# Order hints for a planned kernel: the second tile's tail products behind the first's, a shorter log1p, and a fixed order of the first transfers

## The chip, the core and the metric

The kernel runs on one core of a Trainium2 chip, in one launch. The metric is the device time of that launch in microseconds (us). Five engines work side by side and meet by semaphores: TensorE (PE; its weight loads are shown as PEld), VectorE (DVE), ScalarE (ACT), GpSimd (POOL) and SyncE (SP), whose queue issues every transfer from memory here.

## What is computed

Two transformer blocks run one after the other over a sequence of 256 positions of width 1024, which the kernel holds as two tiles of 128 rows (t = 0 and t = 1). All arithmetic is float32.

```python
def first_block(x, ...):                       # two layers
    for layer in range(2):
        hn = rmsnorm(h, gains[0])
        mix = mixer_ab(hn, ...) if layer == 0 else mixer_c(hn, ...)
        h = h + rmsnorm(mix, gains[1])
        hn = rmsnorm(h, gains[2])
        ff = square(relu(hn @ w_up)) @ w_down
        h = h + rmsnorm(ff, gains[3])
        h = h + sigmoid(h @ w_ple_gate) * (p @ w_ple)

def second_block(x, mem, ...):                 # two layers
    for l in range(2):
        h = rmsnorm(x) @ w_in                  # five kinds of attention
        ... decay = cumsum(log_sigmoid(fox_f + fox_b_f)) ...
        x = x + concat(o_a, o_b, o_c, o_d, o_e) @ w_o
        xn = rmsnorm(x)
        x = x + (silu(causal_dwconv(xn @ w_gate)) * (xn @ w_up)) @ w_down
```

In `mixer_ab` the gates need softplus and log-sigmoid, both through log(1 + e^-|y|).

## The kernel before, in words

Each weight matrix is read in blocks of up to 1 MB into one of two `raw` buffers. `block` splits a block into a rounded part `hi` and a rest `lo` (ACT or DVE copies `hi`, DVE subtracts to get `lo`, in four parts each), which live in four buffers of each kind. A float32 product is then three PE products: `tmm` multiplies a 128-column slice of the block with the transposed activations `aTh`, `aTl` of both tiles at once (256 columns), `nmm` multiplies one tile's activations with 512 columns of the block, for one or two PSUM banks (two banks are the two halves of a 1024-wide result).

Nothing runs in the order in which the code is written. `Recorder.note` collects every instruction with the instructions it depends on; `Recorder.order` ranks them and `arrange` places them on the engines by an estimated cost of each and by waits between engines (`LAG`); `issue` writes each engine's instructions out in that order. On the chip each engine goes through its list in order and waits where an operand isn't there. So a dependency that is added in the recorder adds no wait on the chip: it changes the order alone.

The stages, with the names that matter below:

- Start: `h[0]`, `h[1]` (the two tiles of x), a gain row `g0`, the constants `cf` (its first 128 columns are the identity, with which PE transposes), the columns `cols`, the masks `cb`, `rows` and `pos` are loaded. `normed_T` scales the tiles (DVE, ACT, POOL) and transposes them into `aTh`/`aTl`. The first products are those of the blocks `w0g` (the gates) and `w0t` (ten blocks).
- `mixer_ab`: `gates` makes decay factors from the w0g product on DVE and ACT; `delta` solves triangular systems by a long chain of small products; `w0n` and at last the output matrix `w0o` follow.
- `stream` runs a list `seq` of (block, tile) steps. For an output matrix the list is `tail_lagged(n, tail)`: both tiles for the first n - tail blocks, then the last `tail` blocks for tile 0, then the same blocks for tile 1. `done` is called when a tile's last product is recorded, and spawns what follows it. The gate matrices `wg` use `lagged(4, 2)`, where tile 1 runs two blocks behind tile 0.
- `pre_ff1` (after w0o and w1o): mean square of the tile's result, residual, scaling, four transposes of each half into `aT`. `ff1`: the blocks `wu` and `wd` by turns; when a tile's `wd` sums are complete, `post` does mean square, root, residual and the transposes of `h`; then come the products of `wg`.
- `mixer_c` with `w1n`, `w1o`; `ff1` again; `mixers2` (five attentions, blocks `wi`, `wm`, memory products `wk`, output `wo`) and `ff2` (`fg`, `fu`, `fd`), twice.

In names of the trace and of the orders a number is the tile buffer's; almost every instruction is recorded by one line (L613).

Of the kernel before, what the change touches and what calls it, by code (L numbers as in the profile page):

```python
# [15 lines left out]
OP = mybir.AluOpType  # L16
AX = mybir.AxisListType.X

P = 128
# [53 lines left out]
CF = {}  # L73
# [184 lines left out]
class Recorder:  # L258
# [7 lines left out]
           "act": {"pe": 271, "act": 160, "dve": 142, "pool": 155, "sp": 1220},  # L266
           "dve": {"pe": 270, "act": 128, "dve": 127, "pool": 155, "sp": 1220},
           "pool": {"pe": 200, "act": 90, "dve": 69, "pool": 97, "sp": 1220},
           "sp": dict.fromkeys(("pe", "act", "dve", "pool", "sp"), 2050)}

    def __init__(self, nc):
        self.engines = {"pe": nc.tensor, "act": nc.scalar, "dve": nc.vector, "pool": nc.gpsimd, "sp": nc.sync}
        self.ops, self.pools, self.tile_pool, self.seen = [], {}, {}, {}
        self.run = None


    @contextmanager
    def together(self, share=1):

        self.run = []  # L280
        yield
        op = self.ops[self.run[0]]
        op.cost = op.cost / share + 200 * (share > 1)
        self.run = None

    def engine(self, name):
        rec = self
# [53 lines left out]
    def note(self, eng, call, args, kwargs):  # L341
        op = Op()
        op.eng, op.call, op.args, op.kwargs = eng, call, args, kwargs
        op.preds, op.succs, op.tiles, op.alt, op.more = {}, [], [], None, []
        op.table = self.TABLES.get(args[2], 0) if call == "activation" and args[2] != AF.Copy else None
        isap = lambda x: hasattr(x, "tensor") or hasattr(x, "tag_meta")
        outs = [kwargs[k] for k in ("out", "accum_out") if k in kwargs and isap(kwargs[k])]
        ins = [v for k, v in kwargs.items() if k not in ("out", "accum_out") and isap(v)]
        rest = [a for a in args if isap(a)]
        if "out" not in kwargs:  # L350
            outs.append(rest.pop(0))
        op.cost, op.lag = self.price(op, outs[-1], rest + ins), self.LAG[eng]
        if self.run:
            i = self.run[0]
            first = self.ops[i]
            first.more.append((call, args, kwargs))
            first.cost += op.cost
            op = first
        else:
            i = len(self.ops)  # L360
            self.ops.append(op)
            if self.run is not None:
# [298 lines left out]
def program(ctx, tc, A, out, dbg=None):  # L661
# [157 lines left out]
    def stream(name, items, acts, kpb, halves_, n, seq, done, before=None):  # L819


        first, last = {}, {}
        for t in range(2):
            for i, tt in seq:
                if tt == t:
                    first.setdefault((items[i][0], t), i)
                    last[items[i][0], t] = i
        banks, live = {}, {}
        w = halves_ * n
        for i, t in seq:  # L830
            c, b, k0 = items[i]
            if i not in live:
                live[i] = block(name, b, kpb, w)
            if before is not None:
                before(items[i], t)
            if (c, t) not in banks:
                banks[c, t] = [acc() for _ in range(halves_)]
            hi, lo = live[i]
            for j in range(kpb):
                nmm(banks[c, t], acts(t, k0 + j), hi[:, j, :], lo[:, j, :],  # L840
                    first[c, t] == i and j == 0, last[c, t] == i and j == kpb - 1, n)
                if (j + 1) * 3 * halves_ % 6 == 0:
                    loom.step()
            if last[c, t] == i:
                done(c, t, banks.pop((c, t)))

    def a_T(t, k):
# [248 lines left out]
        put(values_T(pTs, v, ns, heads))  # L1096


    def mixer_ab(end):
        nab = gain(14)  # L1100
        done = {}
        st = {}

        def gates(bank):
# [6 lines left out]
            act.activation(e, e, AF.Exp)  # L1111
            dve.tensor_scalar(u, e, 1.0, None, op0=OP.add)
            act.activation(ln, u, AF.Ln)
            dve.tensor_scalar(u, u, -1.0, None, op0=OP.add)
            dve.scalar_tensor_tensor(z, u, 0.0, e, op0=OP.is_equal, op1=OP.mult)
            dve.tensor_scalar(u, u, 1e-30, None, op0=OP.max)
            dve.reciprocal(u, u)
            dve.tensor_tensor(ln, ln, e, op=OP.mult)
            dve.tensor_tensor(ln, ln, u, op=OP.mult)
            dve.tensor_tensor(ln, ln, z, op=OP.add)  # L1120
            dve.scalar_tensor_tensor(ln, y, 0.0, ln, op0=OP.max, op1=OP.add)
            ca = small(1)
            act.activation(ca, col("alog"), AF.Exp)
# [256 lines left out]
                done[2 + hp, t] = pair_T(flat(m))  # L1380


        hi, lo = block("w0g", 0, 8, P)
        gbank = wk(2)
        tmm(gbank, hi, lo, 1)
        loom.spawn(gates(gbank), "gates")
# [4 lines left out]

        st["nrm"] = wk()
        for bi in W0T:
            hi, lo = block("w0t", bi, 8, 256)
            ps = wk(2)
            tmm(ps, hi, lo)
            if bi >= 6:
# [3 lines left out]
            if bi == 3:  # L1401
                loom.join(*[("conv", i) for i in range(4)], "gates")
                for hp in range(2):
                    g2 = small(4)
                    dve.tensor_copy(g2[:, 0:2], st["eg", 1][:, 2 * hp : 2 * hp + 2])
                    dve.tensor_copy(g2[:, 2:4], st["eg", 1][:, 2 * hp : 2 * hp + 2])
                    st["eg2", hp] = g2
                loom.spawn(norms(), "norms")

        def nat_done(c, t, banks):  # L1410
            b = banks[0]
# [26 lines left out]
            loom.join(*([("B", j - 2)] if j >= 2 else [("A", j, t)]))  # L1438

        items = [(0, j, 2 * j) for j in (2, 3, 0, 1)]  # L1440
        stream("w0o", items, lambda t, k: done[k // 2, t](k % 2), 2, 2, 512, tail_lagged(4, 2), end, before)


    def mixer_c(r, end):
# [32 lines left out]
        def nat_done(c, t, banks):  # L1477
# [5 lines left out]
        stream("w1o", items, lambda t, k: done[k // 2, t](k % 2), 2, 2, 512, tail_lagged(4, 2), end,  # L1483
               lambda it, t: loom.join(("C", it[1], t)))


# [209 lines left out]
    def mixers2(l, r, e, mem, tab, lam, end):  # L1696
# [70 lines left out]
        def forget():  # L1767
# [8 lines left out]
            dve.tensor_scalar(u, u, -1.0, None, op0=OP.add)  # L1776
            dve.scalar_tensor_tensor(z, u, 0.0, e, op0=OP.is_equal, op1=OP.mult)
            dve.tensor_scalar(u, u, 1e-30, None, op0=OP.max)
            dve.reciprocal(u, u)
            dve.tensor_tensor(ln, ln, e, op=OP.mult)  # L1780
            dve.tensor_tensor(ln, ln, u, op=OP.mult)
            dve.tensor_tensor(ln, ln, z, op=OP.add)
            dve.scalar_tensor_tensor(lg, y, 0.0, ln, op0=OP.min, op1=OP.subtract)
            yield
            yield
# [246 lines left out]
        return tabC, tabS, cos_, sin_  # L2032


    sp.dma_start(out=h[0], in_=A["x"][0])
    g0 = gain(0)
    sp.dma_start(out=cf, in_=A["cf"])
    sp.dma_start(out=h[1], in_=A["x"][1])
    loom.spawn(normed_T(0, g0))
    loom.spawn(normed_T(1, g0))  # L2040
    sp.dma_start(out=cols, in_=A["cols"])
    sp.dma_start(out=cb, in_=A["cb"])
    sp.dma_start(out=rows, in_=A["rows"])
    sp.dma_start(out=pos, in_=A["pos"])
    loom.drain()
    tabC, tabS, cos_, sin_ = tables()


    e = [None, None]
# [5 lines left out]
            g2.append(gain(2))  # L2055
        loom.spawn(pre_ff1(0, t, banks, g1[0], g2[0], e), ("pre", 0, t))

    mixer_ab(out0)
    loom.drain()
    dumph("m0")  # L2060

# [99 lines left out]
```

## Time and profile before

| | |
|---|---|
| time, median of 3 runs | 1399.25 us (1395.28 to 1400.75) |
| the profiled execution's own time | 1395.2 us |
| its span, first to last instruction | 1393.4 us |
| mean granted TensorE clock | 0.996 of 2.4 GHz |
| PE busy | 1359.3 us, 98% of the span |
| DVE, ACT, POOL busy | 998.3, 786.4, 56.4 us |

The profile is of one execution. The time of an execution is 1.8 us more than its span, which covers only the program's instructions. PE's busy time is a union of modelled intervals; products overlap in the engine, so the time that a product costs is read from one start to the next.

### The profile page before, as it was taken

The numbers are of one execution on the slowest core, as the hardware profiler recorded it, in microseconds if no ns is written. First come the engines' busy times: TensorE is split into PE (matmuls) and PEld (weight loads), VectorE is DVE, ScalarE is ACT, GpSimd is POOL, SyncE is SP. The second block draws the span as 40 slices with busy tenths as digits, with TensorE's granted clock in tenths as the row PEclk, the third lists the DMA queues.
The fourth block names the chain that finished last, engine by engine and source line by source line (L and its number), as shares of the span: only waits on it lengthen the run. The fifth ranks groups of instructions, "written<-read, shape, count | busy, mean of one in ns | idle before, by whom it ended". The sixth has DMA issues, their size and how long they took to land.

```text
span 1393.4 us, 23108 instructions
## 1 busy us (share of the span) xinstructions
PE 1359.3 (98%) x8768; PEld 1199.4 (86%) x8774; DVE 998.3 (72%) x2417; ACT 786.4 (56%) x1800; POOL 56.4 (4%) x93
## 2 busy tenths in 40 slices
PE   6999999999999999999999999999999999999998
PEld 6899889999787799998787877999998877899997
DVE  6994876666677876566789798575767999576664
ACT  6665554444554854445576596454546679364443
POOL 0000210000010010000020000000001000000000
PEclk9999999999999999999999999999999999999999
DMA  8332354445543364445555243454545523345553
GB/s 329 134 126 99 114 212 182 182 184 194 212 147 141 139 224 179 185 182 194 207 193 206 91 142 132 152 211 153 212 155 205 187 90 99 144 153 210 182 189 114
DMA packets 36400, 236.36 MB, mean 170 GB/s; under 512 B 4160, under 2 KB 4416, under 8 KB 10176
## 3 DMA queue, kind: packets, MB, share of 16 engines
q1 hardware_dynamic: 36288, 234.88, 46.4%
q8 instruction: 69, 1.13, 0.3%
q14 instruction: 43, 0.35, 0.1%
HBM read 233.82 MB, written 1.05 MB: 169 GB/s over the span
## 4 chain that ended last, share of the span: by engine, by line
PE 88%; DVE 6%; ACT 4%; issue 1%; DMA 1%; SPq 0%; POOLq 0%; POOL 0%; ACTq 0%; DVEq 0%
PE ps L613 88%; ACT w L613 3%; DVE w L613 3%; DVE s L613 2%; DMA cf<-in_cf 1%; DVE lo L613 1%; ACT hi L613 1%; DVE h L613 0%; ACT L613 0%; SPq L613 0%; POOLq L2157 0%; DVE hi L613 0%; ACT aTh L613 0%; POOL s L613 0%; ACTq L613 0%
## 5 line engine op out<-in xcount | busy, mean ns | idle before, releaser
L613 ACT ACTIVATE hi<-raw 128x512 fp32r<-128x512 f32 (+1 forms) x793 | 437.6, 620 | 297.7 <-PE ps L613 244.9
L613 DVE TENSOR_TENSOR lo<-raw,hi 128x512 fp32r<-128x512 f32 (+1 forms) x844 | 526.0, 678 | 51.4 <-ACT hi L613 48.1
L613 PE MATMUL ps<-hi,w 128*128 128x512 f32 (+1 forms) x1272 | 379.1, 395 | 0.5 <-ACT w L613 0.5
L613 PE MATMUL ps<-aTl,hi 128*128 128x256 f32 x1256 | 316.7, 280 | 0.0
L613 PE MATMUL ps<-aTh,hi 128*128 128x256 f32 x1256 | 316.3, 281 | 0.0
L613 PE MATMUL ps<-aTh,lo 128*128 128x256 f32 x1256 | 312.5, 280 | 0.0
L613 PEld LDWEIGHTS ps<-hi,w 128*128 128x128 f32 x1272 | 225.2, 188 | 36.1 <-issue 1.9
L613 PEld LDWEIGHTS ps<-aTh,hi 128*128 128x128 f32 x1256 | 224.8, 188 | 9.4 <-ACT hi L613 0.4
L613 PEld LDWEIGHTS ps<-aTl,hi 128*128 128x128 f32 x1256 | 225.1, 188 | 8.3 <-issue 0.4
L613 PEld LDWEIGHTS ps<-aTh,lo 128*128 128x128 f32 x1256 | 223.6, 189 | 9.9 <-DVE lo L613 1.0
L613 PE MATMUL ps<-lo,w 128*128 128x512 f32 (+1 forms) x636 | 205.9, 393 | 0.0
L613 ACT ACTIVATE w<-ps 128x512 f32<-128x512 f32 (+3 forms) x261 | 128.3, 535 | 130.4 <-PE ps L613 119.9
L613 PE MATMUL ps<-hi,aTh 128*128 128x512 f32 (+2 forms) x480 | 148.4, 366 | 3.7 <-ACT w L613 2.5
L613 DVE CAST hi<-raw 128x512 fp32r<-128x512 f32 x51 | 21.8, 427 | 177.8 <-PE ps L613 177.8
L613 PE MATMUL ps<-lo,aTh 128*128 128x512 f32 (+2 forms) x480 | 147.2, 365 | 0.0
L613 PE MATMUL ps<-hi,aTl 128*128 128x512 f32 (+2 forms) x480 | 147.2, 365 | 0.0
L613 ACT ACTIVATE w<-w 128x512 fp32r<-128x512 f32 (+5 forms) x143 | 74.9, 535 | 95.3 <-DVE w L613 93.0
L613 PEld LDWEIGHTS ps<-lo,w 128*128 128x128 f32 x636 | 112.6, 188 | 17.0 <-issue 0.8
L613 PE MATMUL ps<-cf,w 128*128 128x128 f32 (+1 forms) x572 | 94.7, 279 | 17.4 <-DMA cf<-in_cf 10.6
L613 PE MATMUL ps<-w,w 128*64 128x128 f32 (+10 forms) x912 | 109.5, 299 | 0.6 <-ACT w L613 0.5
L613 PEld LDWEIGHTS ps<-w,w 128*128 128x128 f32 (+4 forms) x912 | 88.7, 171 | 20.0 <-ACT w L613 7.4
L613 PEld LDWEIGHTS ps<-hi,aTh 128*128 128x128 f32 x480 | 86.8, 190 | 16.2 <-ACT w L613 2.8
(105 smaller groups left out, 1143.8 us busy)
## 6 DMA issues: line engine op xcount, KB each, us to landing
raw<-in_wu SPq DMA_DIRECT2D x32, 1024.0 KB, 4.8
raw<-in_wd SPq DMA_DIRECT2D x32, 1024.0 KB, 5.0
raw<-in_fg SPq DMA_DIRECT2D x22, 1024.0 KB, 4.8
raw<-in_fu SPq DMA_DIRECT2D x22, 1024.0 KB, 4.8
raw<-in_fd SPq DMA_DIRECT2D x22, 1024.0 KB, 4.8
raw<-in_wi SPq DMA_DIRECT2D x20, 1024.0 KB, 4.8
raw<-in_w0t SPq DMA_DIRECT2D x10, 1024.0 KB, 5.5
raw<-in_wo SPq DMA_DIRECT2D x10, 1024.0 KB, 4.8
```

The source lines that it names most:

```text
L613: getattr(self.engines[op.eng], call)(*args, **kwargs)
```

## The change

Four things are edited. (1) The recorder gets `behind(*ops)`: whatever is recorded inside depends, for the order, on the named instructions. In `stream` with a single group of columns, PE products of tile 1 recorded after tile 0's last step stand behind the instruction recorded last at that point. The tails of w0o and w1o are 3 blocks long, not 2. (2) log1p by another formula: with u = 1 + e, log(u) + (u - 1 - e)(e/2 - 1), without a reciprocal. (3) The first transfers stand in a fixed order: the identity's columns of `cf` by themselves, x, the gain, w0g, the first w0t, `cols`, the rest of `cf`; `cb` after the second w0t, `rows`, `pos` and the gain of mixer_ab after the w0t blocks. (4) The rotary tables are recorded after mixer_ab.

```diff
-           "sp": dict.fromkeys(("pe", "act", "dve", "pool", "sp"), 2050)}
+           "sp": {"pe": 2050, "act": 2050, "dve": 2050, "pool": 2050, "sp": 0}}
...
+    @contextmanager
+    def behind(self, *ops, only=None):
+
+        self.hold, self.only = ops, only
+        yield
+        self.hold = ()
+
+    def last(self):
+        return len(self.ops) - 1
...
+            if self.hold and self.only in (None, eng):
+                op.preds.update(dict.fromkeys(self.hold, True))
...
             for j in range(kpb):
-                nmm(banks[c, t], acts(t, k0 + j), hi[:, j, :], lo[:, j, :],
-                    first[c, t] == i and j == 0, last[c, t] == i and j == kpb - 1, n)
+                with rec.behind(*(ended if t else ()), only="pe"):
+                    nmm(banks[c, t], acts(t, k0 + j), hi[:, j, :], lo[:, j, :],
+                        first[c, t] == i and j == 0, last[c, t] == i and j == kpb - 1, n)
                 if (j + 1) * 3 * halves_ % 6 == 0:
                     loom.step()
             if last[c, t] == i:
+                if t == 0 and len(last) == 2:
+                    ended.append(rec.last())
                 done(c, t, banks.pop((c, t)))
...
-            dve.tensor_scalar(u, u, -1.0, None, op0=OP.add)
-            dve.scalar_tensor_tensor(z, u, 0.0, e, op0=OP.is_equal, op1=OP.mult)
-            dve.tensor_scalar(u, u, 1e-30, None, op0=OP.max)
-            dve.reciprocal(u, u)
-            dve.tensor_tensor(ln, ln, e, op=OP.mult)
-            dve.tensor_tensor(ln, ln, u, op=OP.mult)
-            dve.tensor_tensor(ln, ln, z, op=OP.add)
+
+            dve.scalar_tensor_tensor(u, u, -1.0, e, op0=OP.add, op1=OP.subtract)
+            dve.tensor_scalar(z, e, 0.5, -1.0, op0=OP.mult, op1=OP.add)
+            dve.tensor_tensor(u, u, z, op=OP.mult)
+            dve.tensor_tensor(ln, ln, u, op=OP.add)
...
-        stream("w0o", items, lambda t, k: done[k // 2, t](k % 2), 2, 2, 512, tail_lagged(4, 2), end, before)
+        stream("w0o", items, lambda t, k: done[k // 2, t](k % 2), 2, 2, 512, tail_lagged(4, 3), end, before)
...
-    sp.dma_start(out=h[0], in_=A["x"][0])
-    g0 = gain(0)
-    sp.dma_start(out=cf, in_=A["cf"])
-    sp.dma_start(out=h[1], in_=A["x"][1])
+
+    at = CF["ident"][0]
+    sp.dma_start(out=cf[:, at : at + P], in_=A["cf"][:, at : at + P])
+    with rec.behind(rec.last()):
+        sp.dma_start(out=h[0], in_=A["x"][0])
+    with rec.behind(rec.last()):
+        sp.dma_start(out=h[1], in_=A["x"][1])
+    with rec.behind(rec.last()):
+        g0 = gain(0)
...
+    for name, w in (("w0g", P), ("w0t", 256)):
+        with rec.behind(load[-1], only="sp"):
+            first.append(block(name, 0, 8, w))
```

The same four lines replace the seven in `gates` (256 columns) and in `forget` (8 columns, once in each layer of the second block).

The order of the transfers on SP at the start, before. `raw` is a weight block; with two `raw` buffers the third `raw` row waits until a buffer is read out.

```order
L613 DMA h_81<-in_x 128x1024
L613 DMA h_82<-in_x 128x1024
L613 DMA gb_88<-in_gb 128x1024
L613 DMA raw_142<-in_w0t 128x2048
L613 DMA cf<-in_cf 128x449
L613 DMA raw_117<-in_w0g 128x1024
L613 DMA cols<-in_cols 128x263
L613 DMA cb<-in_cb 128x3456
L613 DMA gb_116<-in_gb 128x1024
L613 DMA gb_489<-in_gb 128x1024
L613 DMA raw_148<-in_w0t 128x2048
```

And of the change:

```order
L627 DMA cf<-in_cf 128x128
L627 DMA h_81<-in_x 128x1024
L627 DMA h_82<-in_x 128x1024
L627 DMA gb_88<-in_gb 128x1024
L627 DMA raw_107<-in_w0g 128x1024
L627 DMA raw_110<-in_w0t 128x2048
L627 DMA cols<-in_cols 128x263
L627 DMA cf<-in_cf 128x321
L627 DMA gb_480<-in_gb 128x1024
L627 DMA gb_481<-in_gb 128x1024
L627 DMA raw_138<-in_w0t 128x2048
```

The identity went from fifth place to first, the w0g block from sixth to fifth, ahead of the first w0t block, and the masks `cb` left the stretch.

PE's order at the end of the first `ff1`, before: ps_537 and ps_538 are tile 0's sums of the down products, ps_539 and ps_540 tile 1's; a row `ps<-cf,h_82 x4` is four transposes of tile 1's h, `h_81` of tile 0's; ps_757 is the first bank of the gate products that follow.

```order
L613 MATMUL ps_539<-hi_725,w_720 128x512
L613 MATMUL ps_537<-hi_725,w_719 128x512
L613 MATMUL ps_538<-hi_725,w_719 128x512
L613 MATMUL ps_537<-lo_726,w_719 128x512
L613 MATMUL ps_537<-hi_725,w_720 128x512
L613 MATMUL ps_538<-lo_726,w_719 128x512
L613 MATMUL ps_538<-hi_725,w_720 128x512
L613 MATMUL ps_744<-cf,h_82 128x128 x4
L613 MATMUL ps_745<-cf,h_82 128x128 x4
L613 MATMUL ps_735<-cf,h_81 128x128 x4
L613 MATMUL ps_757<-hi_747,aTh 128x512
```

And of the change; the line of dots stands for 28 further products of ps_539 and ps_540, and no other row.

```order
L627 MATMUL ps_538<-hi_725,w_720 128x512
L627 MATMUL ps_537<-hi_725,w_720 128x512
L627 MATMUL ps_539<-hi_711,w_697 128x512
L627 MATMUL ps_540<-hi_711,w_697 128x512
...
L627 MATMUL ps_539<-hi_725,w_719 128x512
L627 MATMUL ps_540<-hi_725,w_719 128x512
L627 MATMUL ps_735<-cf,h_81 128x128 x4
L627 MATMUL ps_539<-lo_726,w_719 128x512
L627 MATMUL ps_540<-lo_726,w_719 128x512
L627 MATMUL ps_539<-hi_725,w_720 128x512
L627 MATMUL ps_540<-hi_725,w_720 128x512
L627 MATMUL ps_736<-cf,h_81 128x128 x4
```

Before, both tiles' sums end within nine products and the transposes stand right behind; in the change 32 products of tile 1 stand between tile 0's last product and its transposes. At the end of the second `ff1` it is the same with other numbers.

PE's order at the end of w0o, before: ps_476 and ps_477 are the halves of tile 0's result, ps_478 and ps_479 of tile 1's; ps_529 to ps_534 are products of `wp`, the block that comes next; the transposes of w_498 need tile 0's residual and scaling.

```order
L613 MATMUL ps_477<-hi_487,w_367 128x512
L613 MATMUL ps_478<-lo_488,w_386 128x512
L613 MATMUL ps_478<-hi_487,w_386 128x512
L613 MATMUL ps_479<-hi_487,w_386 128x512 x2
L613 MATMUL ps_479<-lo_488,w_386 128x512
L613 MATMUL ps_479<-hi_487,w_386 128x512
L613 MATMUL ps_533<-hi_527,w_524 128x512
...
L613 MATMUL ps_530<-hi_527,w_525 128x512
L613 MATMUL ps_500<-cf,w_498 128x128 x4
```

And of the change: ps_467 and ps_468 are tile 0's halves (the last product of ps_468 stands 80 products and four transposes further up), ps_469 and ps_470 are tile 1's.

```order
L627 MATMUL ps_467<-hi_478,w_358 128x512
L627 MATMUL ps_470<-hi_478,w_377 128x512
L627 MATMUL ps_469<-lo_479,w_377 128x512
L627 MATMUL ps_469<-hi_478,w_377 128x512
L627 MATMUL ps_470<-lo_479,w_377 128x512
L627 MATMUL ps_470<-hi_478,w_377 128x512
L627 MATMUL ps_529<-hi_527,w_524 128x512
...
L627 MATMUL ps_534<-hi_527,w_525 128x512
L627 MATMUL ps_491<-cf,w_489 128x128 x4
```

Tile 0's last product is followed by 24 products before the transposes in the one, by 29 in the other. The instruction recorded last, which the held products stand behind, is a product of one half (ps_468); the other half (ps_467) still lies among tile 1's products.

## Rows read from the trace of the kernel before

**Rows 1.** The page: its head, and part 1 (busy time, share, instructions).

```profile
span 1393.4 us, 23108 instructions
PE 1359.3 (98%) x8768; PEld 1199.4 (86%) x8774; DVE 998.3 (72%) x2417; ACT 786.4 (56%) x1800; POOL 56.4 (4%) x93
```

**Rows 2.** Sum of three windows of the attention stages: 440:480, 780:860, 1120:1180; busy us.

```profile
sum 180.00, PE 176.18 PEld 135.65 DVE 162.24 ACT 148.35 POOL 1.83; mean PE 58.73 PEld 45.22 DVE 54.08 ACT 49.45 POOL 0.61
```

**Rows 3.** Timeline of SP at the start: start, duration, what is issued.

```profile
0.72 0.86 SPq L613 DMA_DIRECT2D h<-in_x  x2
...
13.13 0.33 SPq L613 DMA_DIRECT2D raw<-in_w0t  x1
```

**Rows 4.** DMA issues of 0 to 14 us: KB each, us from issue to landing.

```profile
cf<-in_cf SPq DMA_DIRECT2D x1, 224.5 KB, 7.9
```

**Rows 5.** DMA issues of 12 to 14 us.

```profile
raw<-in_w0t SPq DMA_DIRECT2D x1, 1024.0 KB, 6.6
```

**Rows 6.** The page, part 6: weight blocks in the middle of the program.

```profile
raw<-in_wu SPq DMA_DIRECT2D x32, 1024.0 KB, 4.8
```

**Rows 7.** Timeline of PE, 0 to 14.5 us; in brackets idle before and releaser.

```profile
10.64 3.65 PE L613 MATMUL ps<-cf,w 128*128 128x128 f32 x16 [10.64 <-DMA cf<-in_cf]
13.94 0.68 PE L613 MATMUL ps<-aTh,hi 128*128 128x256 f32 x2
```

**Rows 8.** Timeline of PE, 57 to 61.6 us, where the gates' chain begins.

```profile
56.83 0.28 PE L613 MATMUL ps<-aTh,hi 128*128 128x256 f32 x1
...
57.06 0.28 PE L613 MATMUL ps<-aTh,lo 128*128 128x256 f32 x1
...
59.93 1.13 PE L613 MATMUL ps<-w,cf 128*128 128x256 f32 x4 [0.87 <-ACT w L613]
```

**Rows 9.** Timeline of DVE at the start and in the gates.

```profile
7.57 2.74 DVE L613 SCALAR_TENSOR_TENSOR w<-h,s,gb 128x512 f32<-128x512 f32 x4 [1.94 <-DMA gb<-in_gb]
...
51.79 1.73 DVE L613 RECIPROCAL w<-w 128x256 f32<-128x256 f32 x1
```

**Rows 10.** Timeline of ACT at the second w0t block and in the gates.

```profile
19.74 2.20 ACT L613 ACTIVATE hi<-raw 128x512 fp32r<-128x512 f32 x4 [4.35 <-DMA raw<-in_w0t]
...
47.55 1.28 ACT L613 ACT_TABLE_LOAD   x1
48.84 0.42 ACT L613 ACTIVATE w<-w 128x256 f32<-128x256 f32 x1
```

**Rows 11.** Timeline of PE at the end of w0o.

```profile
191.37 1.07 PE L613 MATMUL ps<-hi,w 128*128 128x512 f32 x4
192.28 0.61 PE L613 MATMUL ps<-lo,w 128*128 128x512 f32 x2
192.73 0.61 PE L613 MATMUL ps<-hi,w 128*128 128x512 f32 x2
195.14 0.63 PE L613 MATMUL ps<-cf,w 128*128 128x128 f32 x4 [1.79 <-DVE w L613]
```

**Rows 12.** Timeline of PE at the ends of both ff1.

```profile
377.12 0.39 PE L613 MATMUL ps<-hi,w 128*128 128x512 f32 x1
380.86 1.51 PE L613 MATMUL ps<-cf,h 128*128 128x128 f32 x6 [3.35 <-issue]
...
680.09 0.39 PE L613 MATMUL ps<-hi,w 128*128 128x512 f32 x1
683.89 2.37 PE L613 MATMUL ps<-cf,h 128*128 128x128 f32 x10 [3.41 <-DVE h L613]
```

**Rows 13.** Windows of PE behind three waits: us, PE busy, granted clock, DMA share, GB/s.

```profile
380.86:388.00 7.14, 7.14 (x28) 0.61 0.23 73
683.89:688.00 4.11, 4.11 (x21) 0.64 0.55 191
...
759.56:764.00 4.44, 4.44 (x19) 1.00 1.00 387
```

**Rows 14.** Timeline of PE in the first attention layer.

```profile
759.56 0.50 PE L613 MATMUL ps<-hi,aTh 128*128 128x512 f32 x1 [2.52 <-ACT w L613]
```

More of the change, by code (lines that the diff above doesn't have):

```diff
@@ L273, in __init__ @@
         self.ops, self.pools, self.tile_pool, self.seen = [], {}, {}, {}
-        self.run = None
+        self.run, self.hold, self.loads = None, (), []
     @contextmanager
@@ L361, in note @@
             self.ops.append(op)
+            if self.hold and self.only in (None, eng):
+                op.preds.update(dict.fromkeys(self.hold, True))
+            if eng == "sp":
+                self.loads.append(i)
             if self.run is not None:
@@ L827, in stream @@
                     last[items[i][0], t] = i
[L828 removed]
+        banks, live, ended = {}, {}, []
         w = halves_ * n
@@ L1096, in attention, with mixer_ab @@
         put(values_T(pTs, v, ns, heads))
-    def mixer_ab(end):
-        nab = gain(14)
+    def mixer_ab(first, end):
         done = {}
@@ L1380, in mlstm @@
                 done[2 + hp, t] = pair_T(flat(m))
-        hi, lo = block("w0g", 0, 8, P)
+        hi, lo = first[0]
         gbank = wk(2)
@@ L1393, in mixer_ab @@
         for bi in W0T:
-            hi, lo = block("w0t", bi, 8, 256)
+            hi, lo = first[1] if bi == 0 else block("w0t", bi, 8, 256)
+            if bi == 1:
+                with rec.behind(rec.loads[-1]):
+                    sp.dma_start(out=cb, in_=A["cb"])
             ps = wk(2)
@@ L1408, in mixer_ab @@
                 loom.spawn(norms(), "norms")
+        with rec.behind(rec.loads[-1]):
+            sp.dma_start(out=rows, in_=A["rows"])
+            sp.dma_start(out=pos, in_=A["pos"])
+            nab = gain(14)
         def nat_done(c, t, banks):
@@ L1482, in mixer_c @@
         items = [(0, j, 2 * j) for j in range(4)]
-        stream("w1o", items, lambda t, k: done[k // 2, t](k % 2), 2, 2, 512, tail_lagged(4, 2), end,
+        stream("w1o", items, lambda t, k: done[k // 2, t](k % 2), 2, 2, 512, tail_lagged(4, 3), end,
                lambda it, t: loom.join(("C", it[1], t)))
@@ L1775, in forget @@
             act.activation(ln, u, AF.Ln)
[L1776 to L1782, printed above, removed]
+            dve.scalar_tensor_tensor(u, u, -1.0, e, op0=OP.add, op1=OP.subtract)
+            dve.tensor_scalar(z, e, 0.5, -1.0, op0=OP.mult, op1=OP.add)
+            dve.tensor_tensor(u, u, z, op=OP.mult)
+            dve.tensor_tensor(ln, ln, u, op=OP.add)
             dve.scalar_tensor_tensor(lg, y, 0.0, ln, op0=OP.min, op1=OP.subtract)
@@ L2032, in tables @@
         return tabC, tabS, cos_, sin_
-    sp.dma_start(out=h[0], in_=A["x"][0])
-    g0 = gain(0)
-    sp.dma_start(out=cf, in_=A["cf"])
-    sp.dma_start(out=h[1], in_=A["x"][1])
+    at = CF["ident"][0]
[6 more added lines that the diff above has]
+        g0 = gain(0)
+    load = [rec.last()]
     loom.spawn(normed_T(0, g0))
     loom.spawn(normed_T(1, g0))
[L2041 to L2044, printed above, removed]
+    first = []
+    for name, w in (("w0g", P), ("w0t", 256)):
+        with rec.behind(load[-1], only="sp"):
+            first.append(block(name, 0, 8, w))
+        load.append(rec.loads[-1])
+    with rec.behind(load[-1]):
+        sp.dma_start(out=cols, in_=A["cols"])
+    with rec.behind(rec.last()):
+        sp.dma_start(out=cf[:, at + P :], in_=A["cf"][:, at + P :])
     loom.drain()
-    tabC, tabS, cos_, sin_ = tables()
     e = [None, None]
@@ L2056, in out0 @@
         loom.spawn(pre_ff1(0, t, banks, g1[0], g2[0], e), ("pre", 0, t))
-    mixer_ab(out0)
+    mixer_ab(first, out0)
+    tabC, tabS, cos_, sin_ = tables()
     loom.drain()
```

## The prediction

> **What bounds the kernel now.** The head of the page comes first: PE is busy for 1359.3 of 1393.4 us, no other engine for more than 998.3 [rows 1]. The reader is to see that only about 34 us of the span are PE waits, so a change of order can win no more than these waits, and what they do to the clock; the products themselves are the same in both programs. The next view is therefore PE's timeline, read for the bracketed waits. The larger ones stand in five kinds of place.
>
> - The start: transposes wait until 10.64 for `cf`, the first product begins at 13.94 [rows 7].
> - The gates' chain after 57 us: 0.87 and some smaller ones [rows 8].
> - The end of w0o: the last products start at 192.73, the transposes at 195.14 [rows 11]. A product of 512 columns takes (192.28 − 191.37)/4 = 0.2275, so the two end at 193.19 and PE waits 1.95.
> - The ends of the two `ff1`: the last product, issued at 377.12, ends at 377.35, the transposes start at 380.86, a wait of 3.51; the same at 680.09 and 683.89, a wait of 3.57 [rows 12]. Behind them PE has work at once but not the clock: the granted mean is 0.61 over 7.14 us and 0.64 over 4.11 [rows 13], the lower level of 1.2 GHz for most of it. At 0.61, 7.14 us do the work of 4.36, so 2.78 are lost; at 0.64, 1.48. Behind the wait of 2.52 at 759.56 [rows 14] the clock stayed at 1.00 [rows 13], so a shorter wait there lost only itself.
> - The attention stages: in 180 us PE is busy for 176.18 [rows 2], 3.8 idle in many small pieces, with DVE at 90%.
>
> **The change part by part.** The sum is made against the profiled execution's own 1395.2 us.
>
> *Second tile behind the first.* At the first `ff1`, tile 0's last product and its transposes stood six products apart; they now have 32 between them, 32 × 0.2275 = 7.28 us. The chain (square, root, residual) needed 6 × 0.2275 + 3.51 = 4.87 from tile 0's last product. So tile 0's wait goes, and with it the reason for the half clock. What is late next is tile 1: its last product is followed by four of tile 0's transposes (about 0.1 each at the full clock, half of the 3.30/16 at the start [rows 7]) and 16 products of `wg` (3.64), some 4.04 us in all. With 4.87 needed 0.9 remains. Term: −3.5 − 2.8 + 0.9 = −5.4. Bounds: −6.3 if one tile's chain alone is shorter than two that share DVE and ACT, −2 if tile 1's wait is longer and the clock goes down again. At the second `ff1` eight products of cover become 28 (6.37 us), need 8 × 0.2275 + 3.57 = 5.39; tile 1 then has 21 products and four transposes, 5.18, so 0.2 remains: −3.6 − 1.5 + 0.2 = −4.9 (−5 to −2).
>
> At the end of w0o the edit does less than it says: only one half of tile 0's result is finished early. The other half ends 29 products before the transposes instead of 24: 6.60 us of cover against a need of 24 × 0.2275 + 1.95 = 7.41, so at most 0.8 of the 1.95 remains, and less if the early half's share of the chain is done by then. I take −1.5 (−1.95 to 0). At w1o no wait of this kind stood before, at the ends of `wo` I see the same number of products or a few less behind the chain; 0 (0 to +0.3).
>
> In the attention stages, the products still left on PE when the last attention operation comes fall from 48 to 34 (w1o) and from 36 to 27 (each wo): more of them are spread among the attention's operations, which fills some of the 3.8 idle. I take −1.5 (−3.8 to 0). The wait of 2.52 at 759.56 is for a copy that ACT has queued behind other work; nothing in the edits is aimed at it, but the order around it shifts: 0 (−2.5 to +3).
>
> *log1p.* DVE loses the reciprocal, 1.73 [rows 9], and two operations of three in balance, about 2.4 us once, and far less where eight columns are wide. The chain of the gates gets shorter by as much. It is hidden: DVE works on it while PE runs w0t's products until 57.17. In the new order it stands some 10 us earlier and the small products of `delta` follow with fewer large ones between them, so waits like the 0.87 [rows 8] can become less or more. 0 (−1.6, all waits of this place gone, to +2.5, as many again and half). The trace has two table loads fewer to come (1.28 each), on ACT, which PE rarely waits for.
>
> *Transfers.* Before, `cf` landed 7.9 us after its issue [rows 4], ready 10.5, and the transposes began at 10.64. DVE had begun scaling at 7.57, when the gain landed, and its four scalings last 2.74, to 10.31 [rows 9]. With the identity ahead, everything behind it is issued one slot later, 0.43 (half of the 0.86 for the two h) [rows 3]: the gain lands at about 7.9 to 8.0, scaling starts then, the first transposes can start a scaling later, at about 8.7, but the last scaling ends at 10.7, and after its four transposes (3.30/16 each [rows 7], 0.8) and the copies to `aTh`/`aTl` the first product comes at 12.5 to 13.2: 0.8 to 1.5 earlier than 13.94. This is not yet time saved, because the third block decides. Before, it was issued at 13.13, when the first `raw` had been read [rows 3], came 6.6 later [rows 5], and its first split began at 19.74 [rows 10], while PE had 72 products (24 of w0g, 48 of the first w0t) of (57.06 − 56.83)/2 = 0.115 [rows 8], that is work until 13.94 + 8.3 = 22.2. So there 2 us of slack hid it. In the change the first `raw` is w0g's, and by DVE's new order its last rests come after 4 scalings, 4 `aTl`, 4 rests of 512 columns and 4 of 256: 12 × 0.69 + 4 × 0.35 = 9.6 us from 7.9, at 17.4. Only then can the third block be issued; it lands at 22.2 with the 4.8 of a block in mid-program [rows 6], at 24.0 with the 6.6 seen here, plus about 0.5 for a first quarter's split (2.20/4 [rows 10]): 22.7 to 24.5, against the 22.2 at which PE took it before. So the earlier start is given back and more: +1.2 (0.4 to 2.3 by these; −1 if PE finds the block there and keeps its early start, +4 if a later block is late too). `cb`, `rows` and `pos` have no user before the mixers' masks, tens of us later; their move only clears the queue.
>
> By the Trainium skill (DMA: Bandwidth & Descriptors, Measured) a transfer of 64 KB, which the identity is, takes 0.95 us and is mostly overhead, so that the start would by that page lose another 0.5 beside the 0.43 of an issue slot; no row here shows a transfer so small.
>
> ACT's new order has, between the second and the fourth block's split, an exponential, a table load, a logarithm and another table load. In the trace the next ACTIVATE starts right behind a load, 47.55 + 1.28 to 48.84 [rows 10]. I estimate the split of w0t's fourth block at 34.5 and PE's need of it at 35, so it just fits. The Trainium skill (ScalarE: Activation LUTs, What ACT_TABLE_LOAD costs) counts a drain of about 1.38 beside each load; by that page the two loads would put this split 2.8 later and the start's term at about +3.5. The row speaks against it.
>
> The sum: +1.2 (start) + 0 (gates, delta) − 1.5 (w0o) − 5.4 − 4.9 (ff1) + 0 (759) − 1.5 (attention) = −12.1, so 1383.1 for an execution like the profiled one. The median of the three runs lies 4 above it, the lowest run at it; I put the new median at 2 above: 1385.
>
> **Rivals.**
>
> *B, the wait changes tile.* Tile 1's transposes stand behind only 4.04 and 5.18 us of work. If its chain takes clearly longer than the 4.87 to 5.39 read above, since ACT and DVE now put the next blocks' splits between its steps, PE waits there instead, and past a wait like 3.5 the clock falls too. For it: a chain of two tiles was that long while sharing engines, and one tile alone still needs every step. Against it: the old wait came with 1.37 us of cover, the new cover is three times that. Both `ff1` terms then shrink from −10.3 to about −1: 1395.2 − 2.8 = 1392.4, a median of 1394.
>
> *C, the slower one: the held products are missing among the attention operations.* In w1o and both wo, tile 1's held products are 36, 24 and 24, that is 84 × 0.2275 = 19.1 us of PE work that may no longer lie under DVE and ACT, 90% busy there [rows 2]. If the three stages all ran uncovered, and each then lost a clock as at 380 (2.8), the price is 27: 1395.2 − 12.1 + 27 = 1410. It decides from an added idle of 12 in these stages on. Against it: the fewer products left behind the last attention operation, as counted above.
>
> *D, the start costs more.* If the third block lands late and `delta`'s steps, closer together now, wait for each other, the start's and the gates' bounds add up: +4 and +2.5 instead of +1.2, 1388.4, median 1390 to 1391. ACT alone can do it: if it stood still behind each of the two table loads as long as a load lasts (1.28 [rows 10]), the fourth block's split would come at 37 instead of 34.5, 2 later than PE needs it. The drain of the page above is this case.
>
> *E, the new order of the transfers does nothing* is inside the forecast: the start is one of its small terms.
>
> **How the numbers follow.** The forecast has 0.6: 1376 to 1390 as its own range, from the `ff1` terms at −11.3 and the attention at −3.8 on the one side, w0o at 0 and the start at +4 on the other. B has 0.18, D 0.13, C 0.09. The range given is 1376 to 1397: it takes in B and D and leaves out most of C and a little below. A measurement of this kernel can tell some 0.5%, 7 us, from no change, so faster means under 1392.3. The forecast and most of D are faster, B is the same, of C a third is the same: faster 0.71, same 0.21, slower 0.08.
>
> **What would show it.** Right: in PE's timeline no wait over 1 us ahead of the transposes of `h` at both `ff1` ends, a granted clock of 1.00 in the windows behind them, one wait under 1 at the end of w0o, a first product near 13, and a wait of about 1 ahead of the second w0t block near 21 to 24 with the split released by DMA. Wrong: a wait of over 3 before the transposes of tile 1 (B); PE idle above 15 us in the attention stages (C); a second late block or a row of waits at the small products between 40 and 70 us (D). The forecast fails too if the median moves while the two `ff1` ends look as before.

## The result and the profile after

The changed kernel takes 1382.38 us in the median of four runs (1381.70 to 1383.06), the kernel before 1397.84 (four runs, 1395.28 to 1400.75): a ratio of 0.9889, 95% interval 0.9866 to 0.9911. The forecast was 1385.

The head of the page after, against [rows 1]: the span is 13.5 us shorter, PE is busy for 3.6 us less with the same products (part of before was at the lower clock).

```profile
span 1379.9 us, 23087 instructions
PE 1355.7 (98%) x8767; PEld 1195.7 (87%) x8774; DVE 1003.9 (73%) x2423; ACT 785.3 (57%) x1793; POOL 42.8 (3%) x83
```

The waits of PE's timeline, grouped by what they waited for (us in all, times, the longest), first of before, then of after:

```profile
PE ps L613 <- DMA cf<-in_cf: 10.6, 1, 10.6
PE ps L613 <- ACT w L613: 6.6, 13, 2.5
PE ps L613 <- DVE w L613: 3.9, 3, 1.8
PE ps L613 <- issue: 3.8, 4, 3.3
PE ps L613 <- DVE h L613: 3.4, 1, 3.4
...
```

```profile
PE ps L627 <- DVE w L627: 11.7, 2, 8.7
PE ps L627 <- ACT w L627: 3.4, 6, 1.1
PE ps L627 <- DVE lo L627: 2.5, 5, 1.6
PE ps L627 <- DVE aTl L627: 1.8, 3, 0.6
...
```

The line of dots stands for the smallest row of each (1.2 for `aTh` before, 0.2 of "issue" after). The first row of each list holds the start (10.6 before, 8.7 after). Without it the waits fell from 18.9 to 10.9 us. The 3.3 of "issue" and the 3.4 of "DVE h" were the two `ff1` ends [rows 12]; after, neither place has such a wait. Of the 11.7 of after, the 3.0 beyond the start are one wait, behind wo1, which was shorter before.

PE's timeline of after at the first `ff1` end: tile 0's transposes, in two groups of four, lie between products, with no bracket.

```profile
377.23 1.07 PE L627 MATMUL ps<-hi,w 128*128 128x512 f32 x4
378.14 0.60 PE L627 MATMUL ps<-cf,h 128*128 128x128 f32 x4
378.50 0.71 PE L627 MATMUL ps<-lo,w 128*128 128x512 f32 x2
379.05 0.63 PE L627 MATMUL ps<-hi,w 128*128 128x512 f32 x2
379.52 0.60 PE L627 MATMUL ps<-cf,h 128*128 128x128 f32 x4
```

Windows of PE after both ends (us, busy, granted clock, DMA share, GB/s): 2.4 GHz throughout, where [rows 13] had 0.61 and 0.64. The 0.62 idle at the second end is a wait for `aTl` behind tile 0's transposes.

```profile
372.00:382.00 10.00, 10.00 (x49) 1.00 0.33 118
382.00:390.00 8.00, 8.00 (x38) 1.00 0.82 311
670.00:680.00 10.00, 9.38 (x46) 1.00 0.69 229
680.00:690.00 10.00, 10.00 (x49) 1.00 0.68 239
```

The start of after, on PE [rows 7] and in the issues of SP [rows 3]: the transposes wait for DVE's scaling, not for the constants, and begin at 8.73; the first product comes at 12.24; at 23.55 PE has run out of split blocks.

```profile
8.73 3.67 PE L627 MATMUL ps<-cf,w 128*128 128x128 f32 x16 [8.73 <-DVE w L627]
12.24 1.10 PE L627 MATMUL ps<-aTh,hi 128*128 128x256 f32 x2
...
23.55 0.39 PE L627 MATMUL ps<-aTh,lo 128*128 128x256 f32 x1 [1.61 <-DVE lo L627]
...
47.70 1.03 PE L627 MATMUL ps<-w,cf 128*8 128x256 f32 x4 [1.12 <-ACT w L627]
49.18 1.10 PE L627 MATMUL ps<-w,cf 128*128 128x256 f32 x4 [0.45 <-ACT w L627]
...
56.41 1.95 PE L627 MATMUL ps<-w,cf 128*128 128x256 f32 x7 [0.57 <-ACT w L627]
```

```profile
0.72 0.38 SPq L627 DMA_DIRECT2D cf<-in_cf  x1
...
15.94 1.33 SPq L627 DMA_DIRECT2D raw<-in_w0t  x2
```

And behind wo1 the wait has grown; first before, then after:

```profile
1200.97 1.29 PE L613 MATMUL ps<-cf,w 128*128 128x128 f32 x8 [1.54 <-DVE w L613]
```

```profile
1187.50 1.73 PE L627 MATMUL ps<-cf,w 128*128 128x128 f32 x7 [2.94 <-DVE w L627]
```

There the clock went too. A window of PE behind this wait shows 0.52, the lower level, where before had 1.00 behind the shorter one (1200.97 to 1204):

```profile
1187.50:1191.00 3.50, 3.50 (x17) 0.52 0.02 7
```

**Equal work.** To place the difference, each PE instruction was given the median start-to-start time of its form in the kernel before; the times at which two kernels have reached the same sum are compared. Change minus before, in us, by stretches of the kernel before:

| stretch (us of before) | part | change in it |
|---|---|---|
| 0 to 86 | start, gates, delta | +2.2 (−1.9 at the first transpose, +0.7 at 32, +3.8 at 54) |
| 187 to 209 | end of w0o | −0.7 |
| 369 to 404 | first ff1 end | −6.1 |
| 404 to 435 | wg and behind | −0.8 |
| 435 to 510 | w1 mixer, w1o | −2.2 |
| 671 to 685 | second ff1 end | −4.0 |
| 754 to 767 | the wait at 759 | −2.9 |
| 767 to 864 | attention, wo0 end | −2.7 |
| 864 to 884 | behind wo0 | +2.1 |
| 1074 to 1124 | ff2 end, second attention's start | +1.8 |
| 1124 to 1198 | second attention | −2.3 |
| 1198 to 1212 | wo1 end | +1.3 |
| the rest | | +1.1 |

The sum is −13.2, close to the 13.5 by which the spans differ.

### The profile page after: what moved, and what is told of

The parts are those of the page before. It is cut to its first block, busy times and chain, and to the rows that moved or that the text cites. A ratio compares the mean times of both kernels' runs of the same rounds, so it can differ in the third digit from the quotient of the medians.

```text
span 1379.9 us, 23087 instructions
## 1 busy us (share of the span) xinstructions
PE 1355.7 (98%) x8767; PEld 1195.7 (87%) x8774; DVE 1003.9 (73%) x2423; ACT 785.3 (57%) x1793; POOL 42.8 (3%) x83
## 4 chain that ended last, share of the span: by engine, by line
PE 88%; DVE 9%; ACT 2%; DMA 1%; issue 1%; SPq 0%; DVEq 0%; ACTq 0%
PE ps L627 88%; DVE w L627 3%; DVE lo L627 3%; DVE s L627 2%; ACT w L627 1%; DMA gb<-in_gb 0%; DVE h L627 0%; DMA raw<-in_wu 0%; ACT hi L627 0%; ACT L627 0%; DVE aTl L627 0%; DVE hi L627 0%; SPq L627 0%; DVE tab L627 0%; ACT aTh L627 0%
## 5 line engine op out<-in xcount | busy, mean ns | idle before, releaser
L627 ACT ACTIVATE hi<-raw 128x512 fp32r<-128x512 f32 (+3 forms) x787 | 431.6, 619 | 287.5 <-PE ps L627 239.3
L627 DVE TENSOR_TENSOR lo<-raw,hi 128x512 fp32r<-128x512 f32 (+2 forms) x844 | 525.4, 679 | 36.8 <-ACT hi L627 33.7
L627 PE MATMUL ps<-aTh,hi 128*128 128x256 f32 x1256 | 333.6, 281 | 0.3
L627 PE MATMUL ps<-aTh,lo 128*128 128x256 f32 x1256 | 330.9, 281 | 2.3 <-DVE lo L627 2.3
L627 PE MATMUL ps<-aTl,hi 128*128 128x256 f32 x1256 | 331.1, 280 | 0.6 <-DVE aTl L627 0.6
L627 PEld LDWEIGHTS ps<-aTh,lo 128*128 128x128 f32 x1256 | 227.5, 189 | 12.5 <-DVE lo L627 3.1
L627 PE MATMUL ps<-lo,w 128*128 128x512 f32 x636 | 216.7, 395 | 0.0
L627 ACT ACTIVATE w<-ps 128x512 f32<-128x512 f32 (+2 forms) x261 | 127.1, 518 | 125.0 <-PE ps L627 119.0
L627 PE MATMUL ps<-hi,aTh 128*128 128x512 f32 (+2 forms) x480 | 159.0, 371 | 0.1
L627 ACT ACTIVATE w<-w 128x512 f32<-128x512 f32 (+5 forms) x144 | 75.9, 534 | 107.4 <-DVE w L627 106.9
L627 PE MATMUL ps<-cf,w 128*128 128x128 f32 (+1 forms) x572 | 101.0, 281 | 12.9 <-DVE w L627 11.7
L627 PEld LDWEIGHTS ps<-hi,aTl 128*128 128x128 f32 x480 | 86.5, 188 | 13.3 <-DVE aTl L627 1.1
```

The lines of the kernel that those rows point to most:

```text
L627: getattr(self.engines[op.eng], call)(*args, **kwargs)
```

## The experiments

All were timed in five rounds against the kernel before on the same chip; its median there was 1395.9 to 1398.1.

**Parts alone.** The four edits were separated. `e1_hold_only` puts the hold and the tails of 3 on the kernel before (the last two lines, in w0o and in w1o, are cut to the argument that changes):

```diff
+                if t == 0 and len(last) == 2:
+                    ended.append(rec.last())
...
-tail_lagged(4, 2)
+tail_lagged(4, 3)
```

> The kernel before with the hold in the streams and the tails of 3 blocks; old log1p, old start, tables in their old place. Theory A, the gain comes from the hold, and the new start costs: the change's gain without the +2.0 us that its profile shows by 65 us, so 1379 to 1382 and a ratio to before of 0.987, the waits of 3.5 at both ff1 ends gone. Rival B, the separation at the ff1 ends is a by-product of the other parts: 1392 or more, both waits still there.

Measured: 1378.14, ratio 0.9864 (0.9850 to 0.9877). Theory A, 0.9 under its range. The hold alone is faster than the whole change: its slowest run (1379.84) lies under the change's fastest (1381.70).

`e2_start_only` has the new transfers and the moved tables, without hold, tails and log1p.

> The kernel before with the fixed order of the first transfers and the tables after the first mixer; no hold, tails of 2, old log1p. Theory A: PE is 1 to 3 us later than in before once the gates and delta are done (at equal work near 70 us), and nothing else moves: 1398 to 1401. Rival B: 1390 or less. Rival C, the start gives 1.9 us and the loss came with the moved log1p: 1395 to 1397.

Measured: 1404.07, ratio 1.0042 (1.0028 to 1.0056): the sign of A, three times its size. PE waits 1.87 at 24 us and 1.55 and 1.78 at 47 and 53, and here the clock goes too:

```profile
24.00:34.00 10.00, 9.66 (x71) 0.83 0.68 251
54.00:70.00 16.00, 14.57 (x95) 0.89 0.34 132
```

By these mean clocks that is 1.7 + 1.8 us on top of the waits. By equal work 6.9 us are lost by 75 us. The profile loses 1.5 and 1.6 more near 690 and 760: the waits there are those of before (3.41 and 2.52), but the clock behind them is lower for longer (0.69 from 692 to 700, 0.79 from 767 to 775). So "nothing else moves" did not hold.

`e3_log1p_only` exchanges the formula alone.

> The kernel before with the shorter log1p alone. Theory A: hidden under PE, 1397 to 1399, the same; in the profile the gates' DVE work is 2.4 us shorter and the waits at 58 to 65 us together shrink by at most 1.6. Rival: it was worth the whole 2.4, 1395.5.

Measured: 1395.35, ratio 0.9985 (0.9977 to 0.9994), 1.7 less: the rival's number, but not by its reason. It isn't the gates: by equal work it is 0.8 later at 369 us, gains 1.0 at the first `ff1` end, where the wait is the same (3.34) and the clock is back at 1.00 from 385 on, and 2.4 at the wait of [rows 14], which is gone. There the shorter `forget` has changed the order; PE's only wait at this place is now

```profile
757.67 0.44 PE L613 MATMUL ps<-cf,w 128*128 128x128 f32 x2 [0.16 <-ACT w L613]
```

`e6_start_log1p` is the change without the hold's line (in the order as written out, tails of 3 without it change nothing; no run has them alone), `e5_hold_log1p` the change without its new start.

```diff
-                if t == 0 and len(last) == 2:
-                    ended.append(rec.last())
```

> The change without the hold (the new start and the short log1p; the tails of 3 alone leave the order as it was). Theory A, the 7.0 us that the new start cost by itself were the gates' chain, 10 us earlier and without cover, and the short log1p takes some 5 of them back: 1397.0 + 2 less the 2.3 of the wait in the first attention layer that went with log1p alone: 1396 to 1400. Rival, the parts add: 1397.0 + 7.0 - 1.7 = 1402.

Measured: 1398.13, ratio 1.0000 (0.9990 to 1.0010). The parts don't add: the short log1p takes back more than its own 1.7 of the start's 7.0, as A said. Of the wait near 24 us 1.73 is left, the waits of 47 and 53 are gone.

> The change without its new start: hold, tails of 3 and the short log1p on the old order of the transfers, tables in their old place. Theory A, the parts add where they do not touch: 1378.1 (hold alone) less 1.7 (log1p alone), 1375 to 1379, faster than the change. Rival, the short log1p needs the new start or the other way round: 1381 or more.

Measured: 1379.42, ratio 0.9871 (0.9851 to 0.9890), 0.4 above A's range and no difference from the hold alone that these intervals tell. The gain of log1p alone was the wait at 759, and the hold removes that too.

**Why the hold separates the tiles of ff1.** The sums of `ff1` are not made in `stream`, so no product of theirs is held. Two kernels hold in one place each, with tails of 2 and all else of before.

```diff
-                if t == 0 and len(last) == 2:
+                if t == 0 and len(last) == 2 and name.startswith("wg"):
```

> The kernel before with the hold in the wg products alone (tails of 2, all else old). The products of the ff1 sums are in no stream and are held behind nothing. Theory A, a hold further down makes tile 0 more urgent in the ranking and so separates the tiles above it: both waits of 3.5 gone and the clock at 1.00 behind them, 10 to 11 us less, 1387. Rival, a hold moves only the products that it names: both waits still there, 1396 to 1399.

Measured: 1386.23, ratio 0.9920 (0.9908 to 0.9932). Theory A. Windows of PE over both ends:

```profile
370.00:390.00 20.00, 20.00 (x97) 1.00 0.58 215
672.00:692.00 20.00, 19.56 (x93) 1.00 0.66 233
```

In `e8_hold_w1o` the condition is `name == "w1o"`.

> The kernel before with the hold in w1o alone (tails of 2). Theory A, urgency goes up the program from the held products and reaches the next place above: the first ff1 (16 products between tile 0's last product and its transposes, so a wait of about 1 and no half clock there, 4 to 6 us), and not the second, below it (3.57 still there): 1391 to 1393. Rival, it acts at w1o alone: 1396 to 1398; rival, it acts on the whole order: both waits gone, 1387.

Measured: 1393.74, ratio 0.9975 (0.9964 to 0.9985); 0.7 above A's range, but the two sites say what it said. The first end, above w1o, is separated (4.7 us less by equal work from 369 to 404), the second, below, is as it was:

```profile
379.39 1.34 PE L627 MATMUL ps<-cf,h 128*128 128x128 f32 x8 [0.34 <-PE ps L627]
...
679.99 1.18 PE L627 MATMUL ps<-cf,h 128*128 128x128 f32 x7 [3.41 <-DVE h L627]
```

```profile
379.39:388.00 8.61, 8.47 (x42) 1.00 0.45 178
679.99:688.00 8.01, 7.94 (x35) 0.79 0.32 100
```

The reason lies in the code: `order` ranks an instruction by the longest chain of work behind it. Since tile 1's held products can only come after tile 0's, all that leads to tile 0 ranks higher than the same work of tile 1. Both runs fit this, and e8 shows it for the place above and not for the one below; the ranks themselves are in no trace.

**What the half clock costs.** `e7_fill_wait` leaves the order of before and puts 14 idle products into each wait as it is written out.

```diff
+            if i in self.fill:
+                b, w, x = self.fill[i]
+                for _ in range(14):
+                    self.engines["pe"].matmul(b, w, x, start=True, stop=True)
```

> The kernel before, its order unchanged, with 14 extra products of 512 columns (3.2 us, results not used) in each of the two waits at the ff1 ends, between the last product and the transposes. Theory A, the half clock behind these waits costs what the windows say: the clock stays at 1.00, the chain and so the start of the transposes stay where they are, and 2.8 + 1.5 us come back: 1392 to 1394. Rival, PE is held by the chain there and the half clock costs nothing: 1396 to 1398 with the clock at 1.00.

Measured: 1394.83, ratio 0.9980 (0.9971 to 0.9989). The chain hasn't moved: the transposes start 3.46 after the last product has ended (3.51 before):

```profile
376.70 0.39 PE L617 MATMUL ps<-hi,w 128*128 128x512 f32 x1
376.92 3.35 PE L615 MATMUL ps<-aTh 128*128 128x512 f32 x14
380.39 2.00 PE L617 MATMUL ps<-cf,h 128*128 128x128 f32 x12
```

```profile
377.00:389.00 12.00, 11.79 (x59) 1.00 0.27 85
680.00:690.00 10.00, 9.73 (x50) 1.00 0.29 87
```

By equal work, with the idle products not counted, 2.2 and 0.9 us came back behind the two waits, less than the 2.8 and 1.5 that the windows of before gave. The timelines say the same: from the first transpose to the same four products further down it took 390.80 − 380.86 = 9.94 us before and 388.17 − 380.39 = 7.78 in e7.

```profile
390.80 1.08 PE L613 MATMUL ps<-hi,aTh 128*128 128x512 f32 x4
```

```profile
388.17 1.07 PE L617 MATMUL ps<-hi,aTh 128*128 128x512 f32 x4
```

At the lower clock the work didn't take twice as long: the twelve transposes lasted 2.44 us up to the next product's start before (380.86 to 383.30) and 1.75 in e7 (380.39 to 382.14). Then 1.5 were lost again near 760 us. The wait of 2.52 is there as in before [rows 14], but now with the lower clock behind it:

```profile
756.00:759.50 3.50, 3.49 (x9) 0.53 1.02 386
```

The total, 2.8 less by the medians, is short of A's range. The two sites refute the rival and bear A out, but for the size.

**The start and the half that isn't held.** `e9_w0t_first` exchanges w0g and the first w0t.

```diff
-    for name, w in (("w0g", P), ("w0t", 256)):
+    for name, w in (("w0t", 256), ("w0g", P)):
```

> The change with the first w0t block ahead of w0g in the fixed order (on SP a second w0t block then stands before w0g too). Theory A, the start loses because w0g is a short block: PE's work of the two first blocks is 72 products, and the next block can be issued only when w0g has been split; with two w0t blocks first PE has 96 products, the wait of 1.8 near 21 us goes, and the gates' chain has its filler back: 2 to 3 us less than the change, 1379 to 1380.5. Rival, the loss lies in delta's steps wherever they stand: 1382 to 1384.

Measured: 1382.41, ratio 0.9902 (0.9887 to 0.9917): the rival's number. The wait near 21 us went, as A said, but by equal work PE is no less late at 65 us than in the change (2.7 against 2.0), and stands at other places:

```profile
44.10 0.38 PE L627 MATMUL ps<-aTh,lo 128*128 128x256 f32 x1 [1.25 <-DVE lo L627]
...
53.65 1.56 PE L627 MATMUL ps<-w,cf 128*128 128x256 f32 x6 [1.49 <-DVE w L627]
```

That pointed to DVE. `e10_both_halves` is e5 with tile 1 behind both halves of tile 0's sum.

```diff
-                    ended.append(rec.last())
+                    ended.extend(rec.last() - x for x in range(halves_))
```

> The change without its new start, with tile 1 held behind the last products of both halves of tile 0, not of one. Theory A, half a hold is what left the waits of 0.7 after w0o and of 3.1 after wo1: between tile 0's end and its transposes now stand 25 products at wo1 (5.7 us, 8 before): the 3.1 goes to under 1, w0o's wait goes, 1375.5 to 1378 against the 1379.4 with one half. Rival, DVE or ACT are late there for other reasons (weight splits ahead of the chain): 1379 to 1381.

Measured: 1378.01, ratio 0.9868 (0.9854 to 0.9881). At wo1 A holds: the transposes follow the products with no wait, the clock is 1.00 behind them (1184 to 1190), and by equal work 2.5 us are gained on before from 1198 to 1212, where e5 lost 1.1 and the change 1.3.

```profile
1184.86 0.39 PE L627 MATMUL ps<-hi,w 128*128 128x512 f32 x1
1185.09 1.03 PE L627 MATMUL ps<-cf,w 128*128 128x128 f32 x8
```

At w0o nothing is gained. In sum no gain shows: the medians lie 1.4 apart, but before itself was 1.7 faster in the rounds of e10 than in those of e5, and the ratios are 0.9868 and 0.9871. So A is shown at wo1 and not in the total.

`e11_w0t_first_both` has both edits on the change.

> Both of the last two edits on the change: the first w0t block ahead of w0g, tile 1 behind both halves. If both theories hold, and an identity that lands early saves one more us at the start: 1374 to 1377, the fastest so far. If one of them falls: 1378 to 1380.

Measured: 1381.38, ratio 0.9889 (0.9876 to 0.9903). That is outside both forecasts. The gain at wo1 is there (4.7 us against e9), but the start lost 1.8 more; why isn't known.

`e12_gates_late_both` instead holds the gates' first DVE operation behind the last split of the fifth w0t block, where it stands in the kernel before; tile 1 is again behind both halves.

```diff
-        loom.spawn(gates(gbank), "gates")
...
+            if bi == 3:
+                loom.spawn(gates(gbank, rec.last()), "gates")
...
+            with rec.behind(late, only="dve"):
+                dve.tensor_scalar(y, bank[:, 0, :], col("gbias"), col("gsgn"), op0=OP.add, op1=OP.mult)
```

> The change with the gates' first DVE operation held behind the last split of the fifth w0t block (where it stands in the kernel before), and tile 1 held behind both halves. Theory A, what the new start loses between 43 and 57 us is DVE time: DVE is over 92% busy from 24 us on, and the gates' work, now ahead of the w0t splits, lets their buffers come free late and PE run out of products. So the wait near 21 us stays, those of 43 to 57 go, and PE at equal work near 70 us is not later than in the kernel before (2.2 later in the change): 1376.5 to 1379. Rival, the gates and delta cost the same wherever they stand: 2 later at equal work still, 1380 to 1381.5.

Measured: 1377.60, ratio 0.9858 (0.9841 to 0.9874). Windows of all engines (PE, PEld, DVE, ACT, POOL, clock, DMA), first the change, then e12:

```profile
44.00:54.00 10.00, 8.17 (x48) 5.84 (x48) 9.69 (x22) 3.66 (x8) 0.00 (x0) 1.00 0.00 0
```

```profile
44.00:54.00 10.00, 10.00 (x71) 7.57 (x70) 9.80 (x25) 7.83 (x15) 0.00 (x0) 1.00 0.28 99
```

PE is full where it was idle for 1.8 of 10, DVE is as busy in both. By equal work PE at 75 us is 0.7 later than in the kernel before, against 2.1 in the change. What is left is the wait near 24 us (1.82). The run has two edits, but the second one left the start no earlier in the two pairs that differ by it alone (1.8 later from e9 to e11, about 0.3 from e5 to e10), so the gain at the start is put down to the gates. e12, e10 and e1 lie within 0.6 us of each other and can't be ranked by these runs; every run of the three (1376.74 to 1379.84) is below the change's fastest, though they stood beside executions of before whose medians differ by 2.2.

## Why the prediction was right, step by step

- **First ff1 end**, −5.4 forecast: −6.1. The wait and the half clock went, and tile 1's wait of 0.9, the heart of rival B, didn't come: its transposes found their `h` ready. Its cover was reckoned against 4.87, a chain of two tiles that shared DVE and ACT; alone, it had the first half of `h` some 3.5 us after its last product (379.5 to 383.0).
- **Second ff1 end**, −4.9: −4.0, with a new 0.62 for `aTl` and a half clock that was worth 0.9, not 1.5.
- **How this comes about** was not in the prediction: it counted products between rows of the order, and these were right, but it put the separation down to the held products themselves. e4 and e8 show that holds further down are enough for it.
- **The half clock** was priced at 2.8 and 1.5 by the windows; e7 shows 2.2 and 0.9. With these and the waits of 3.5 and 3.6 the two ends come to −5.7 and, with the 0.62, to −3.9, near what was measured.
- **w0o**, −1.5: −0.7. The half hold was seen; its worth was put too high (0.55 of waiting stands there now, for `aTl`). Its other place was missed: at wo1 the second half of tile 0's sum ends late and the wait grew from 1.54 to 2.94, and the clock fell to 0.52 behind it, +1.3 in all where the wo ends were costed at 0 to +0.3. e10 and e11, with both halves held, have neither the wait nor the lower clock, and are faster there than e5 and e9 by 3.6 and 4.7; so the half hold is the cause.
- **The wait at 759**, 0 (−2.5 to +3): −2.9. "The order around it shifts" was right; that it shifts to the good could not be read. It goes as well with log1p alone.
- **Attention stages**, −1.5: with the stretches of the table from 435 to 510, 767 to 884 and 1074 to 1198 the sum is −2.2 − 2.7 + 2.1 + 1.8 − 2.3 = −3.3, gains and losses of up to 2.7 in turn. Rival C fell: it needed 12 us more of idle PE in these stages, and all waits of PE behind 380 us add up to 6.0.
- **Start and gates**, +1.2 and 0: +2.2 together, inside the bounds. The first transposes (8.7) came as worked out, the first product (12.24) 0.3 before its 12.5 to 13.2, and a wait near 21 to 24 came as well (1.61, not about 1). Its cause was half wrong: the third block was issued at 15.94, not 17.4, and landed 4.8 later, at 20.73, earlier than the 22.2 to 24 given; DVE, with six other operations ahead of the block's rests, was late. The gates' 0 was an undersized term: the waits of 1.12, 0.45 and 0.57 at the small products between 47 and 57 us are the sign that rival D named. e2 shows what the gates' place costs with the long log1p, e12 that with the gates later the loss of 43 to 57 us is gone. "It is hidden" was the step that failed: DVE, busy for 9.69 of 10 us there, is the engine in need.
- **The identity and the table loads.** The 64 KB of the identity were issued in 0.38 and had landed 1.9 after their issue began; the gain landed at 7.79 against 7.43, so the start lost 0.36 by it. By the Trainium skill (DMA: Bandwidth & Descriptors, Measured) a transfer of 64 KB takes 0.95, in a table of transfers that GpSimd issues; here SP issued it, and that time isn't seen by itself. The loss of another 0.5 that the prediction estimated from the page did not come. On ACT, in its timeline, the next ACTIVATE starts 1.29 and 1.30 after the start of each of the two new table loads, and the fourth block's split begins at 30.97, not 34.5. So no drain of 1.38 beside a load, as the Trainium skill has it (ScalarE: Activation LUTs, What ACT_TABLE_LOAD costs), stands in this trace.

```profile
27.41 1.28 ACT L627 ACT_TABLE_LOAD   x1
28.70 0.42 ACT L627 ACTIVATE w<-w 128x256 f32<-128x256 f32 x1
29.14 1.28 ACT L627 ACT_TABLE_LOAD   x1
30.44 0.63 ACT L627 ACTIVATE w<-w 128x512 f32<-128x512 f32 x1
30.97 1.14 ACT L627 ACTIVATE hi<-raw 128x512 fp32r<-128x512 f32 x2
```

The errors of the two signs nearly cancel: −12.1 was forecast, −13.5 measured in the profiled executions. That the sum comes so near is in part luck: the 2.9 at 759 and 1.8 more in the attention stages, which nothing in the sum foresaw, pay for the start, w0o, the second `ff1` end and wo1. Nor does the lower end of the forecast's own range follow from the two terms it names: 1385 less 1.0 (`ff1`) and 2.3 (attention) is 1381.7, not 1376, and 1382.38 lies just above it.

## What to carry to other kernels

In a planned program, a dependency added to an order moves more than the work that it names: it raises the rank of all that leads to it, so test a hint alone and read the places above it. Price a wait of PE with the clock behind it, by comparing equal work and not by the window's mean alone, which here gave 2.8 for 2.2 us and 1.5 for 0.9. And an edit that is right by itself (constants earlier, a shorter formula) may cost time when it lets work go early on an engine that is already full: here a start that was 1.9 us earlier ended 2.2 us later.

## What was not expected of the hardware

A wait of 2.52 us at 759 left the granted clock at 1.00 [rows 13, 14]. The same wait, as long and at the same place, has 0.53 behind it in e7 and lower clock behind it in e2 as well, and e2, with waits of at most 1.87 near 24 and 53 us, shows 0.83 and 0.89 behind those. So the length of a wait alone doesn't tell whether the clock falls; what else decides was not tried. It also means that two kernels can differ by 1.5 us at a place that the edit didn't touch. 14 products whose result nobody uses, in a wait that they don't lengthen, kept the clock at 1.00.
